# Turning the gates of a gated attention trunk: VectorE blocks and a trip through DRAM in place of TensorE transposes

## The chip, the core and the metric

The kernel runs on one core of a Trainium2 chip. The metric is the device time of one execution in microseconds (us), the median of several. Engines are named as in the profile: PE is TensorE's matmul, PEld its weight load, DVE is VectorE, ACT is ScalarE, POOL is GpSimd, SP is SyncE, which only issues transfers. ACT and POOL issue transfers too.

## The reference, cut to what matters

One layer over 512 tokens of width 2048. A projection of the normalised input gives, for each of three mixers (A, B, C) and four heads of width 128, a query, a key, a value and a gate. Each mixer computes attention in its own way; the head's output is multiplied by SiLU of the gate, projected up, weighted by sigmoid merge gates, summed and projected out.

```
hn = rmsnorm(x, norm_g)
proj = jnp.einsum('bsd,dc->bsc', hn, w_in)
br = proj[..., :QKVG_COLS].reshape(b, s, N_BRANCH, 4, BRANCH_W)      # q, k, v, gate
gates = jax.nn.sigmoid(proj[..., QKVG_COLS + N_HEADS:] + b_gate)
...
ys = jnp.stack([from_heads(ya), from_heads(yb), from_heads(yc)], axis=2)
ys = ys * jax.nn.silu(br[:, :, :, 3])
up = jnp.einsum('bsnw,nwd->bsnd', ys, w_up)
merged = jnp.sum(gates * up, axis=2)
return x + jnp.einsum('bsd,de->bse', merged, w_out)
```

All of it is float32. The shape of the problem: SEQ = 512, D_MODEL = 2048, three mixers of four heads, HEAD_DIM = 128.

## The kernel before, in words

**Products.** Every float32 product is made of three passes of a faster type: an operand is split into a high half and a low half (`wh` and `wl` for weights), and high x high, high x low and low x high are added up in PSUM. ACT makes the high half of a weight tile by a copy (line 377), DVE the low half by a subtraction (line 385). There are three buffers for `wh` (`LA + 1`) and two for `wl` (`LA`). The matmuls of all big products stand on one line, 266.

**Units.** The work on weights is a list of 405 units, each with one weight tile of 128 x 1024 (the first two have half of it) and 12 or 24 matmuls of 128 x 512. The first 9 units are head (C, 0), its weight columns for q, k, v and gate together; the next 8 a group of merge-gate columns. Then come eleven products in Strassen's form (class `Strassen`), 28 units each: each makes one head's 512 columns and one group of merge-gate columns at once, from seven products over half the tokens. Then the up projection and the output projection. A head's four token blocks `c[tb]` (128 tokens on partitions, 512 columns: q, k, v, gate) are there when its product's units end.

**Stages of a head.** Class `Head` makes attention out of `c`: `norms` (query and key norms on ACT), `qk` (query and key turned so that the head dimension is on partitions), `gate`, `values`, scores, softmax or stick-breaking, `silu` (line 1054) and `av`, in which the head's output is multiplied by the gate. `turned(r)` (line 867) makes four 128 x 128 transposes on PE into one PSUM bank of the `att` pool and returns it. `gate` copies that bank to the tile `g` on ACT (line 919). `stages` (line 1105) says how many units behind the end of the head's product each starts: `gate` at 2, `silu` at 12 or 14, or at 4 for the last head, whose attention has no product of a later head beside it.

**Order.** The order of PE, ACT and DVE is written out by a planner at build time (class `Flow`). Each stage is a generator that yields an engine and an estimated cost, an event to wait for, or a number of slots of a buffer pool. The planner keeps a clock for each of the three engines, takes whichever instruction can start first (by due time among equals), and emits it then. Its clock is an estimate; on the chip each instruction waits for its data by semaphores, and each engine runs its list in order. Transfers are estimated by `landing` (line 271). The issuing engine waits in its own queue for a transfer's source and for its buffer. SP has nearly all loads and stores; POOL has the loads that add to a tile (`add_up`); ACT has the first two `x` tiles and the output's stores.

**Pools.** `t2` tiles (128 x 512 float32, `NT = 20` of them) hold `c`, `g`, `y` and most other intermediate tiles. `raw` has 8 weight tiles as they come from DRAM. `att` has four PSUM banks for attention and turning, `acc` four for products.

**The start.** The input is loaded as 16 tiles `x` (128 x 512); tiles 0 and 1 go out on ACT's queue (line 296), the first weights and the other `x` tiles on SP's, in the order written in `loads` (line 1454): x0, w0, x1, w1, x2, x3, w2 and so on, without x0 and x1. PE runs 36 small matmuls (line 429) until the first weight is there. The first unit's `wh` is made by DVE (line 374).

Of the kernel before, what the change touches and what calls it, by code (L numbers as in the profile page):

```python
# [8 lines left out]
F32 = mybir.dt.float32  # L9
# [6 lines left out]
P = 128  # L16
S = 512
# [6 lines left out]
QB = S // P  # L24
# [12 lines left out]
Q, K, V, G = 0, 1, 2, 3  # L37
PE, ACT, DVE = 0, 1, 2
# [26 lines left out]
class Flow:  # L65
# [16 lines left out]
    def give(self, slots, n=1):  # L82
        slots.free += [self.fin] * n
# [71 lines left out]
def act_us(n, x=1):  # L155
    return x * (0.075 + 0.00095 * n)


def dve_us(n, x=1):
    return x * (0.1 + 0.00105 * n)  # L160
# [3 lines left out]
def hybrid_kernel(  # L164
# [13 lines left out]
    nc = tc.nc  # L178
# [5 lines left out]
    tp = ctx.enter_context(tc.tile_pool(name="tp", bufs=NT))  # L184
    sp = ctx.enter_context(tc.tile_pool(name="sp", bufs=8))
    dp = ctx.enter_context(tc.tile_pool(name="dp", bufs=1, space=bass.MemoryType.DRAM))
# [5 lines left out]
    def nm(s):  # L192
        uid[0] += 1
        return f"{s}_{uid[0]}"

    flow = Flow()
    spawn, set_, give = flow.spawn, flow.set, flow.give
    t2s, atts, raws, xps = Slots(NT, KEPT), Slots(4), Slots(NR), Slots(NX)
    accs, wls = Slots(4), Slots(LA)

    def t2(s, dt=F32):
        return tp.tile([P, S], dt, tag="t2", name=nm(s))
# [10 lines left out]
    def f(ap):  # L213
        return ap.bitcast(F32)

    def blk(i):
        return slice(i * P, (i + 1) * P)
# [53 lines left out]
    def landing(ready, kb):  # L271

        line[0] = max(line[0], ready) + 0.5
        line[1] = max(line[1], line[0] + 1.0) + kb / 370.0
        return line[1] + 1.5

    def fetch(to, src, ready, kb):
        nc.sync.dma_start(to, src)
        return Event(landing(ready, kb))
# [6 lines left out]
    def stored(slots, n, kb):  # L286

        slots.free += [landing(flow.fin, kb)] * n
# [2 lines left out]
    nc.scalar.preload_act_table_set("natural_log_exp_and_others")  # L291
    small_in = cp.tile([P, consts.shape[1]], F32, name="small_in")
    nc.sync.dma_start(small_in, consts)  # L293
    x_first = [tp.tile([P, S], F32, tag="t2", name=nm("x")) for _ in range(2)]
    for i in range(2):
        nc.scalar.dma_start(x_first[i], xT[i])
    gn = small_in[:, 0:KT]
    gqk = small_in[:, KT:KT + 4]
    bfc = small_in[:, KT + 4:KT + 5]
# [68 lines left out]
    def prep(u):  # L368
        n = u.shape[0] * S
        u.hi = wp.tile([P] + u.shape, F32R, tag="wh", name=nm("wh"), bufs=LA + 1)  # L370
        yield u.there
        if u is units[0]:
            yield DVE, dve_us(n)
            nc.vector.tensor_copy(u.hi, u.raw)  # L374
        else:
            yield ACT, act_us(n)
            nc.scalar.activation(u.hi, u.raw, AF.Copy)  # L377
        set_(u.ready_hi)
        if u.prev is not None:
            yield u.prev.took  # L380
        yield wls, 1
        set_(u.took)
        u.lo = wp.tile([P] + u.shape, F32R, tag="wl", name=nm("wl"), bufs=LA)
        yield DVE, dve_us(n)
        nc.vector.tensor_sub(u.lo, u.raw, f(u.hi))  # L385
        set_(u.ready)
        u.split_done()
# [30 lines left out]
    raw_ev = [Event() for _ in range(KT)]  # L418
# [7 lines left out]
    xraw, x_in = [None] * KT, [Event() for _ in range(KT)]  # L426
# [389 lines left out]
    class Head:  # L816
# [95 lines left out]
        def gate(self):  # L912
            yield from self.all_there()
            yield t2s, 1
            yield atts, 1
            ps = yield from self.turned(G)
            yield ACT, act_us(S)
            self.t[G] = t2("g")
            nc.scalar.activation(self.t[G], ps, AF.Copy)
            give(atts)  # L920
            set_(self.event(G))
# [520 lines left out]
    def loads():  # L1442
        def x(kt):
            yield t2s, 1
            if kt < 2:
                xraw[kt], x_in[kt].t = x_first[kt], (3.6, 5.2)[kt]
                return
            xraw[kt] = t2("x")
            x_in[kt].t = fetch(xraw[kt], xT[kt], 0.0, 256).t

        def n(i):
            n_in[i].t = fetch(xnat[i // 2][:, i % 2, :], xn[i // NQ, i % NQ], 0.0, 256).t

        order = [("x", 0), ("w", 0), ("x", 1), ("w", 1), ("x", 2), ("x", 3), ("w", 2)] + [("n", i) for i in range(4)]
        order += [("x", 4), ("x", 5), ("w", 3)] + [("n", i) for i in range(4, 8)]
        order += [("x", 6), ("x", 7), ("w", 4)] + [("n", i) for i in range(8, 12)]
        order += [("x", 8), ("x", 9), ("w", 5)] + [("n", i) for i in range(12, 14)]
        for i in range(6, 9):
            order += [("x", 2 * i - 2), ("x", 2 * i - 1), ("w", i)] + [("n", j) for j in (14, 15) if i == 7]
        for kind, i in order:  # L1460
            if kind == "x":
                yield from x(i)
            elif kind == "n":
                n(i)
            else:
                yield from units[i].load()
        for u in units[9:]:
            yield from u.load()
# [4 lines left out]
    def stream():  # L1473
        for i, u in enumerate(units):
            for g, slack in side.pop(i, ()):
                spawn(g(), slack, flow.fin)
            for j in range(LA + 1) if i == 0 else (i + LA,):
                if j < len(units):
                    spawn(prep(units[j]), 2.5, flow.fin)
            yield u.ready_hi  # L1480
            yield from u.mms(u)
            give(wls)
            if u.after is not None:
                spawn(u.after(), 0.0, flow.fin)
# [70 lines left out]
```

## Time and profile before

| | |
|---|---|
| Median of 3 runs | 1306.08 us (1305.84 to 1307.55) |
| The profiled execution's own time | 1305.88 us |
| Its span, first to last instruction | 1304.2 us |
| Granted TensorE clock | 1.000 |
| PE, PEld, DVE, ACT, POOL busy | 100%, 83%, 82%, 58%, 7% of the span |
| Moved by DMA | 278.64 MB, mean 214 GB/s |

The span lies inside the profiled execution's own time, so 1.7 us of it are before the first and behind the last instruction. A busy share is the union of an engine's instructions; matmuls overlap, so their durations add up to more than their busy time. "idle before <-X" is time in which the engine did nothing, and what ended it. ACTq and SPq are the issuing side of ACT and SP; a transfer's time to landing runs from its issue to its semaphore. Rows of a window give its bounds and length, then busy time of PE, PEld, DVE, ACT and POOL, then the granted clock, the DMA engines' share and GB/s.

### The profile page before, as it was taken

The page shows a single profiled execution, that of the slowest core. Times are in us where ns is not written, and L with a number is a line of the kernel's source. Part 1 is how long each engine was busy: PE and PEld are TensorE (multiplying, and loading weights), DVE is VectorE, ACT ScalarE, POOL GpSimd, SP SyncE. Part 2 cuts the span into 40 slices and gives each one's busy share as a digit, 9 for nine tenths or more (in the row PEclk, how much of TensorE's full clock was granted, in tenths as well). Part 3 has the DMA queues.
Part 4 walks back from the last instruction along what each step waited for, and adds up shares of the span by engine and source line. Part 5 has one row for each costly group of instructions (what it writes and reads, how often), then busy time and mean ns, then how long its engine had stood idle before and what let it go on. Part 6 is the DMA issues. An engine that isn't in the chain of part 4 may idle for free.

```text
span 1304.2 us, 17267 instructions
## 1 busy us (share of the span) xinstructions
PE 1299.0 (100%) x5985; PEld 1078.7 (83%) x5985; DVE 1063.9 (82%) x1563; ACT 753.0 (58%) x1270; POOL 91.6 (7%) x116
## 2 busy tenths in 40 slices
PE   9999999999999999999999999999999999999998
PEld 7888888888888888888888888888888888888887
DVE  7966796998989888898886886878879668698767
ACT  7745464664547656566475664666658545463442
POOL 0001000110011101110011100110000000000110
PEclk9999999999999999999999999999999999999999
DMA  9845668887787878878687776867786756738983
GB/s 363 249 130 141 187 200 208 230 217 216 219 233 235 239 228 258 236 229 241 182 234 172 218 207 181 239 154 210 210 274 201 267 188 190 187 87 257 253 243 128
DMA packets 95033, 278.64 MB, mean 214 GB/s; under 512 B 10960, under 2 KB 11104, under 8 KB 94944
## 3 DMA queue, kind: packets, MB, share of 16 engines
q1 hardware_dynamic: 77376, 218.27, 49.4%
q0 software_dynamic: 14976, 54.53, 22.9%
q10 hardware_dynamic: 2592, 4.72, 1.0%
q8 instruction: 47, 0.77, 0.2%
q14 instruction: 42, 0.34, 0.1%
HBM read 257.77 MB, written 19.71 MB: 213 GB/s over the span
## 4 chain that ended last, share of the span: by engine, by line
PE 99%; DMA 0%; DVE 0%; SPq 0%; issue 0%
PE acc L266 93%; PE att L872 1%; PE att L1000 1%; PE att L1090 1%; PE att L262 1%; PE att L1089 1%; PE att L263 1%; PE att L261 1%; PE att L1088 1%; PE att L1338 1%; DMA raw<-in_w_col 0%; DVE s L701 0%; DVE wh L374 0%; SPq L293 0%; PE att L969 0%
## 5 line engine op out<-in xcount | busy, mean ns | idle before, releaser
L377 ACT ACTIVATE wh<-raw 128x1024 fp32r<-128x1024 f32 (+1 forms) x404 | 426.0, 1056 | 377.0 <-PE acc L266 300.4
L385 DVE TENSOR_TENSOR wl<-raw,wh 128x1024 fp32r<-128x1024 f32 (+1 forms) x405 | 493.2, 1219 | 159.5 <-PE acc L266 104.1
L266 PE MATMUL acc<-wh,x 128*128 128x512 f32 x1664 | 432.3, 393 | 0.4 <-DVE wh L374 0.4
L266 PEld LDWEIGHTS acc<-wh,x 128*128 128x128 f32 x1664 | 308.5, 188 | 62.1 <-issue 0.6
L266 PE MATMUL acc<-wh,t 128*128 128x512 f32 x1056 | 271.8, 390 | 0.0
L266 PEld LDWEIGHTS acc<-wh,t 128*128 128x128 f32 x1056 | 197.2, 188 | 40.4
L266 PE MATMUL acc<-wl,x 128*128 128x512 f32 x832 | 230.6, 391 | 0.0
L266 PEld LDWEIGHTS acc<-wl,x 128*128 128x128 f32 x832 | 155.4, 188 | 32.6 <-DVE wl L385 0.2
L266 PE MATMUL acc<-wl,t 128*128 128x512 f32 x528 | 148.7, 392 | 0.0
L282 POOL DMA_DIRECT2D raw<-in_w_col x88 | 76.1, 865 | 870.5 <-ACT wh L377 177.3
L587 DVE TENSOR_TENSOR raw<-raw,raw 128x1024 f32<-128x1024 f32 x104 | 126.5, 1219 | 0.1
L266 PEld LDWEIGHTS acc<-wl,t 128*128 128x128 f32 x528 | 98.2, 188 | 19.9
L266 PE MATMUL acc<-wh,m 128*128 128x512 f32 x448 | 112.9, 389 | 0.0
L266 PE MATMUL acc<-wh,y 128*128 128x512 f32 x384 | 103.1, 390 | 0.0
L266 PEld LDWEIGHTS acc<-wh,m 128*128 128x128 f32 x448 | 84.1, 188 | 17.5
L266 PEld LDWEIGHTS acc<-wh,y 128*128 128x128 f32 x384 | 71.9, 188 | 15.0
L266 PE MATMUL acc<-wl,m 128*128 128x512 f32 x224 | 62.5, 390 | 0.0
L266 PE MATMUL acc<-wl,y 128*128 128x512 f32 x192 | 59.4, 391 | 0.0
L266 PEld LDWEIGHTS acc<-wl,m 128*128 128x128 f32 x224 | 41.9, 188 | 8.8 <-DVE wl L385 0.2
L266 PEld LDWEIGHTS acc<-wl,y 128*128 128x128 f32 x192 | 35.8, 188 | 7.1
L247 ACT ACTIVATE ah<-att 128x512 fp32r<-128x512 f32 (+3 forms) x48 | 20.9, 435 | 33.8 <-PE att L1000 33.8
L1304 DVE TENSOR_TENSOR sg<-acc,sg 128x512 f32<-128x512 f32 x48 | 32.8, 689 | 5.0 <-PE acc L266 2.6
(179 smaller groups left out, 1129.7 us busy)
## 6 DMA issues: line engine op xcount, KB each, us to landing
raw<-in_w_col SPq DMA_DIRECT2D x235, 512.0 KB, 4.5
raw<-in_w_col POOLq DMA_DIRECT2D x88, 512.0 KB, 8.1
raw<-in_w_out SPq DMA_DIRECT2D x40, 512.0 KB, 4.6
raw<-in_w_up SPq DMA_DIRECT2D x24, 512.0 KB, 4.1
sg<-gl SPq DMA_DIRECT2D x48, 256.0 KB, 5.1
xf<-in_xn SPq DMA_DIRECT2D x32, 256.0 KB, 6.7
raw<-in_w_out POOLq DMA_DIRECT2D x16, 512.0 KB, 5.9
gl<-u SPq DMA_DIRECT2D x22, 256.0 KB, 9.8
```

Of the source, the lines that this page charges most:

```text
L247: nc.scalar.activation(hi, src, AF.Copy)
L261: nc.tensor.matmul(ps, lh, rh, start=start, stop=False, skip_group_check=more)
L262: nc.tensor.matmul(ps, lh, rl, start=False, stop=False, skip_group_check=more)
L263: nc.tensor.matmul(ps, ll, rh, start=False, stop=stop, skip_group_check=more)
L266: nc.tensor.matmul(ps, w, x, start=start, stop=stop, skip_group_check=more)
L282: nc.gpsimd.dma_start(to, src, accum_op=ALU.add)
L377: nc.scalar.activation(u.hi, u.raw, AF.Copy)
L385: nc.vector.tensor_sub(u.lo, u.raw, f(u.hi))
L587: nc.vector.tensor_add(to.raw, to.raw, self.raw)
L872: nc.tensor.transpose(ps[:, blk(tb)], self.c[tb][:, blk(r)], identf)
L1000: nc.tensor.transpose(ps[:, blk(i)], self.p[i][:, blk(j)], identf)
L1304: nc.vector.tensor_mul(t, ps[tb], t)
```

## The change: what it does

For all heads but the last, `gate` no longer uses PE and PSUM. DVE transposes the gate's 128 x 128 part of each token block into a tile `gt`; its instruction turns each 32 x 32 piece where it stands, so the sixteen pieces of a block are turned but not moved. SP stores `gt` to a DRAM tile `gd`, laid out by piece row. The planner then waits 12 us of its clock, and ACT issues four loads, one for each 32 partitions of the tile `g`, which pick the pieces so that each comes to its place: 512 pieces of 512 B in the store, 2048 pieces of 128 B in the four loads of a head, 256 KB each way. The planner counts 0.3 us of DVE for each transpose and 0.2 us of ACT for the four loads, and takes `g` to be there 14 us later. The last head goes the old way.

At the start, ACT's queue has `x` tile 0 alone; tile 1 goes on SP's queue at its place in `loads`, behind the first weight tile. The low half of the first weight is made after the low half of `x` tile 0 (`raw_ev[0]`).

```
-    x_first = [tp.tile([P, S], F32, tag="t2", name=nm("x")) for _ in range(2)]
-    for i in range(2):
-        nc.scalar.dma_start(x_first[i], xT[i])
+    x_first = tp.tile([P, S], F32, tag="t2", name=nm("x"))
+    nc.scalar.dma_start(x_first, xT[0])
...
         if u.prev is not None:
             yield u.prev.took
+        else:
+            yield raw_ev[0]
         yield wls, 1
...
         def gate(self):
             yield from self.all_there()
             yield t2s, 1
+            if not self.last:
+                t = t2("gt")
+                for tb in range(QB):
+                    yield DVE, 0.3
+                    nc.vector.transpose(t[:, blk(tb)], self.c[tb][:, blk(G)])
+                self.taken()
+                gd = dp.tile([4 * QB, 32, P], F32, name=nm("gd"))
+                nc.sync.dma_start(gd.rearrange("(t a) r c -> (a r) t c", a=4), t.rearrange("p (t c) -> p t c", t=QB))
+                stored(t2s, 1, 256)
+                yield Event(flow.fin + 12.0)
+                yield t2s, 1
+                yield ACT, 0.2
+                t = self.t[G] = t2("g")
+                for b in range(4):
+                    nc.scalar.dma_start(t[32 * b:32 * (b + 1), :].rearrange("p (n c) -> p n c", c=32),
+                                        gd.rearrange("n r (b c) -> b r n c", c=32)[b])
+                self.event(G).t = flow.fin + 14.0
+                return
             yield atts, 1
             ps = yield from self.turned(G)
...
-            if kt < 2:
-                xraw[kt], x_in[kt].t = x_first[kt], (3.6, 5.2)[kt]
+            if kt == 0:
+                xraw[0], x_in[0].t = x_first, 3.6
                 return
```

## The prediction

> **What bounds it.** I read the page's busy shares and its chain first, then who TensorE waited for, then the waits of the engines that feed it.
>
> ```profile
> PE 1299.0 (100%) x5985; PEld 1078.7 (83%) x5985; DVE 1063.9 (82%) x1563; ACT 753.0 (58%) x1270; POOL 91.6 (7%) x116
> PE 99%; DMA 0%; DVE 0%; SPq 0%; issue 0%
> ```
>
> The chain that ends last is TensorE's own instruction stream, so time falls where that stream gets shorter, as long as nothing starts to hold it up. Who it waited for in all, and who its feeders waited for (us in total, times, longest):
>
> ```profile
> PE att L429 <- DVE mskf L303: 1.1, 1, 1.1
> PE acc L266 <- DVE wh L374: 0.4, 1, 0.4
> ...
> ACT wh L377 <- PE acc L266: 300.4, 190, 5.7
> ACT wh L377 <- DMA raw<-in_w_col: 36.9, 20, 4.4
> ```
>
> TensorE waited twice, both times before its first product. ScalarE, which makes the high half of each weight tile, stood 190 times because all three wh buffers were full, and it could lose 4.4 us to a late weight without TensorE noticing. So a lead of about 4.4 us stands between a feeder's delay and the time.
>
> **What leaves TensorE.** The chain around one gate (start, length, what), and the copy out of PSUM behind it on ScalarE:
>
> ```profile
> 399.98 8.62 PE acc L266 x38
> 408.59 0.44 PE att L872 x4
> 409.03 5.47 PE acc L266 x24
> ...
> 409.07 0.60 ACT L919 ACTIVATE g<-att 128x512 f32<-128x512 f32 x1 [0.76 <-PE att L872]
> ```
>
> Four transposes take 0.44 us of the chain. Eleven of the twelve heads lose theirs: 11 x 0.44 = 4.84 us, all of it on the path that sets the end. This term I trust most: every group of four in the chain has that length.
>
> A rule puts it higher. The same instruction's duration (min/median/max):
>
> ```profile
> L872 PE MATMUL att<-identf,w x66: 270/271/273, 157.2 to 999.8; 128*128 128x128 f32 x66
> ```
>
> The Trainium skill (TensorE: Matmul & The Clock Gate, Part 4: PE-mode transpose) gives about 275 ns for a 128x128 transpose in a kernel's context. The row agrees with it as a duration; by it 44 transposes would be 12.1 us. The chain speaks against using it as a price: in 0.44 us it passes four of them, because each starts before the one ahead has ended.
>
> **What VectorE gets.** Per head four 32x32-block transposes of a 128x128 piece. The trace has none. The nearest rows of that size are a copy with one input and a subtraction with two:
>
> ```profile
> L316 DVE CAST identb<-identf 128x128 bf16<-128x128 f32 x1 | 0.2, 216 | 0.0
> 169.03 0.28 DVE L908 TENSOR_TENSOR vl<-w,vh 128x128 fp32r<-128x128 f32 x1
> ...
> 653.00:665.00 12.00, 12.00 (x57) 9.94 (x56) 11.93 (x21) 9.58 (x29) 2.28 (x3) 1.00 0.84 222
> ...
> 657.35 1.22 DVE L385 TENSOR_TENSOR wl<-raw,wh 128x1024 fp32r<-128x1024 f32 x1
> ...
> 659.97 0.61 PE L266 MATMUL acc<-wl,x 128*128 128x512 f32 x2
> ```
>
> So 4 x 0.22 to 4 x 0.28 = 0.88 to 1.12 us a head; I take 1.12, since all data is f32. In the 12 us around this gate VectorE is busy 11.93 us (fourth figure of the windows row), so the work isn't free there: what is queued behind it, the low half wl of a weight tile, comes that much later. The wl begun at 657.35 is done at 658.57 and used at 659.97, so 1.40 us are in hand; 1.12 leaves 0.28. I cost it at nothing on the path, covered by that lead. If the lead is gone, all 1.12 us show: 12.3 us over 11 heads.
>
> **What ScalarE gets.** It loses 0.60 us (the copy) and issues four loads a head. Rows of issues: one whose pieces are strided as here, with partitions in groups of 32, one plain, and ScalarE's load about 12 us after a gate.
>
> ```profile
> L783 SPq DMA_DIRECT2D lf<-fd x4: 608/614/749, 635.5 to 637.6; - x4
> ...
> 1289.01 0.34 ACTq L1423 DMA_DIRECT2D out<-u  x1
> ...
> 421.00:433.00 12.00, 12.00 (x58) 10.15 (x57) 8.24 (x18) 4.05 (x6) 0.00 (x0) 1.00 1.03 302
> ```
>
> Four issues take 1.36 to 3.0 us; I take 4 x 0.61 = 2.4, as the strided one is nearest. Net of the copy +1.8 us a head, where the planner has 0.2. At 12 us behind the gate ScalarE is busy 4.05 of 12 us, and queued behind the loads are wh splits with 4.4 us of lead: nothing on the path.
>
> The loads also wait for the store to be in DRAM, and hold ScalarE if it isn't. For stores of the same 256 KB, issue to landing is:
>
> ```profile
> DMA to landing us min/median/max: 2.0/5.4/10.5
> ```
>
> The planner leaves 12 us, 1.5 more than the slowest. The store stands in SyncE's queue in front of later weight loads and waits there for the four VectorE transposes, about the wait for wl that those loads have anyway. The gate is wanted late, as one head's copy and its first use show:
>
> ```profile
> L919 ACT ACTIVATE g<-att x1: 599/599/599, 161.9 to 161.9; 128x512 f32<-128x512 f32 x1
> L1062 ACT ACTIVATE y<-g x1: 622/622/622, 191.7 to 191.7; 128x512 f32<-128x512 f32 x1
> ```
>
> There are 29.8 us in between; store and loads at 12 + 10.5 = 22.5 fit in.
>
> **What the DMA engines get.** 512 pieces of 512 B and 2048 of 128 B a head: on each of 16 engines 32 and 128. The trace has 64 B pieces (the lf loads, in a window of 2.3 us where nothing else ran) and 2 KB ones (queue 10; packets, MB, share of 16 engines):
>
> ```profile
> q1 hardware_dynamic: 148, 0.01, 3.8%
> ...
> q10 hardware_dynamic: 2592, 4.72, 1.0%
> ```
>
> That is 0.038 x 16 x 2300 / 148 = 9.5 ns, and 0.010 x 16 x 1304200 / 2592 = 81 ns. In a straight line between them by size 128 B come to 12 ns and 512 B to 26: 128 x 12 + 32 x 26 = 2.4 us of every engine. Bounds: all at 9.5 give 1.5 us, all at 81 give 13.0. I take 2.4, since the 64 B row is nearest. The 12 us after the pause are full already (DMA share 1.03 in the row above), so weights slip by as much, which the 4.4 us of lead hold. From about 28 ns a piece (160 x 28 = 4.5 us) they no longer do.
>
> **The start.** Timeline of the first microseconds, the window behind it, and the tightest later weight:
>
> ```profile
> 1.13 4.02 PE L429 MATMUL att<-mskf 128*128 128x128 bf16 x36 [1.13 <-DVE mskf L303]
> ...
> 4.93 0.43 DVE L374 CAST wh<-raw 128x512 fp32r<-128x512 f32 x1 [0.94 <-DMA raw<-in_w_col]
> 5.39 0.69 DVE L385 TENSOR_TENSOR wl<-raw,wh 128x512 fp32r<-128x512 f32 x1
> 5.51 2.49 PE L266 MATMUL acc<-wh,x 128*128 128x512 f32 x8 [0.36 <-DVE wh L374]
> ...
> 6.40 1.94 ACT L448 ACTIVATE x<-x,small_in 128x512 fp32r<-128x512 f32 x3
> ...
> 8.76 1.99 PE L266 MATMUL acc<-wh,x 128*128 128x512 f32 x8
> ...
> 5.50:10.00 4.50, 4.49 (x18) 3.60 (x19) 4.44 (x8) 3.77 (x6) 0.01 (x1) 1.00 1.04 399
> ...
> 26.04 1.06 ACT L377 ACTIVATE wh<-raw 128x1024 fp32r<-128x1024 f32 x1 [0.22 <-DMA raw<-in_w_col]
> ...
> 27.81 3.79 PE L266 MATMUL acc<-wh,x 128*128 128x512 f32 x16
> ```
>
> The first product waits for the first weight (the copy at 4.93 waited for its DMA). x tile 1 no longer shares the transfers ahead of that weight; its 256 KB at 399 GB/s are 0.66 us, so the weight lands up to 0.66 us sooner. TensorE's warm-up runs until 1.13 + 4.02 = 5.15, so of that only the idle 0.36 can be won. Moving x tile 1 to SyncE's queue puts it after one weight load, and the second weight and all that follow on that queue one issue (about 0.45) later; their transfers then queue behind full engines anyway, and x tile 1 converts by 7.05 for a product at 8.76. The low half of x tile 0 now precedes wl on VectorE: in the old order it ran from 6.00 to 6.75, now it can run from 5.39; wl ends later, about 6.8, for a use at 7.84. The gain lasts only if no later weight binds: the tightest is done at 27.10 for 27.81, 0.71 us, more than 0.36. I take 0.36, with -0.45 (everything one issue late) and +0.66 as bounds.
>
> **Sum.** 4.84 + 0.36 = 5.2 us. The profiled execution took 1305.88 us (span 1304.2, 1.7 around it), 0.2 under the median of 1306.08. 1305.88 - 5.2 = 1300.7; half of the 0.2 added, 1300.8.
>
> **Rivals.** Late wl, the slower side: VectorE has 0.07 of 12 us free at the gate. The planner's new order may put the transposes ahead of a wl whose lead is under 1.12. It decides from 5.2 / 11 = 0.47 us of TensorE waiting a head; at the full 1.12 the time is 1300.7 + 12.3 = 1313.0. Against it: the 1.40 us, and PE rows without one wait for wl. Chance 0.08.
>
> Pieces dear: if short pieces cost like long ones, 13.0 us a head fall into a stretch where the engines are full, 4.4 are covered, and 11 x 8.6 = 95 us come on top: 1395; at 31 ns a piece it comes out even. Against it stands the 9.5 ns row. The Trainium skill (VectorE: DVE Perf Modes, The three transpose paths) warns that a plain DMA that transposes by its strides is 19 times slower than the crossbar's 1309 ns for 128x128: 25 us a block, 100 a head. Here both sides move runs of 32 elements, and no row of this trace shows such a rate. Chance 0.04.
>
> No gain kept: the 0.44 us a head return as small waits, on a late store (10.5 of 12 us in the worst row) or a wh behind it: 1306, within the bound. For it, the full DMA window behind the gates; against it, that ScalarE idles 8 of 12 us there. A weaker form, half kept, is 1303.3. Chance 0.10 for the first.
>
> More than forecast: each removed transpose worth its 271 ns, 11.9 us: 1293.8. Against it, the 0.44 row. Chance 0.03.
>
> **How the numbers follow.** The forecast, from 1299.9 (start at its upper bound, 0.05 us less around each gate) to 1303.3 (half of it lost), has 0.75. Its 1300.8 is the prediction. The range goes down to 1299.0 and up to 1306.0, to take in the case without gain; the dear pieces and the full wl case lie outside with 0.12. A measurement of this kernel tells 0.2%, 2.6 us, from no change: faster means below 1303.5. Faster 0.75 + 0.03 = 0.78, same 0.10, slower 0.08 + 0.04 = 0.12.
>
> **What will show it.** PE instructions 5985 - 44 = 5941, the chain without its 0.44 us pieces of the eleven gates, and still no TensorE wait after the start: that is the main term. VectorE up by 10 to 12 us in 44 transposes. First product near 5.15 instead of 5.51. ScalarE waits for the store none or under 2 us. Wrong would be waits of acc L266 for wl or wh behind the gates, loads on queue 10 whose pieces take 28 ns or more, or a unit between 5 and 30 us that starts later than before.

## The result and the profile after

| | before | after |
|---|---|---|
| Median | 1306.28 us of 6 runs (1305.84 to 1307.55) | 1301.47 us of 6 runs (1300.12 to 1302.68) |
| Profiled execution, span | 1305.88, 1304.2 us | 1301.76, 1300.1 us |

The ratio is 0.9963, with a 95% interval of 0.9953 to 0.9974: faster by 4.8 us, where 5.3 were forecast. The runs of the changed kernel lie 2.6 us apart, those of the old one 1.7.

The page of the changed kernel, its busy shares, its queue 10 and its chain:

```profile
PE 1294.1 (100%) x5941; PEld 1075.1 (83%) x5941; DVE 1069.5 (82%) x1607; ACT 748.2 (58%) x1259; POOL 92.0 (7%) x116
...
q10 hardware_dynamic: 25680, 7.34, 2.3%
...
PE 99%; DMA 1%; DVE 0%; issue 0%; ACT 0%; ACTq 0%
```

TensorE has the 5941 instructions forecast and 4.9 us less to do (1299.0 before); it is still what the time is made of. The new 1% of DMA in the chain is one wait. Who waited for whom (us in total, times, longest):

```profile
PE att L430 <- DVE mskf L302: 1.1, 1, 1.1
PE att L261 <- ACT p L1049: 0.9, 1, 0.9
...
ACT wh L376 <- PE acc L266: 317.6, 203, 5.7
...
ACT wh L376 <- DMA g<-gd: 13.2, 5, 3.4
```

Behind the start, TensorE waits once, for 0.9 us, which it didn't before. In the `g<-gd` row ScalarE's next wh stands five times behind the loads of `g`. Such an idle time holds the issues of the four loads too, and some are put down to another transfer, as here:

```profile
427.97 1.06 ACT L376 ACTIVATE wh<-raw 128x1024 fp32r<-128x1024 f32 x1 [3.01 <-DMA raw<-in_w_col]
430.26 2.04 ACTq L930 DMA_DIRECT2D g<-gd  x4
432.48 1.06 ACT L376 ACTIVATE wh<-raw 128x1024 fp32r<-128x1024 f32 x1 [3.45 <-DMA gl<-s]
```

Of the 3.45 us, 2.04 are issues, and 1.23 are ScalarE's wait for the store, from 429.03 to 430.26. Head by head that wait is 0.7 to 1.3 us in six heads and nothing in the other five. No TensorE row answers to it.

Two pieces of the chain of waits, around that wait and around a gate (start, length, what):

```profile
330.25 10.56 DMA gl<-u
...
340.89 0.29 ACT p L1049
...
341.23 0.50 PE att L261
...
394.98 23.36 PE acc L266 x103
```

The last row runs through the place where the old chain had four transposes of 0.44 us; here are 103 matmuls without a break. The three rows above it are the wait: a transfer `gl` took 10.56 us from its issue to its landing, ScalarE's `p` stood until its tile was free, and the scores product stood behind it.

To see where the time went, I took the first matmul of each unit in both traces. At each of the eleven gates the distance shrinks by 0.46 to 0.49 us, in sum 5.2; the wait at 341 us gives back 1.2 by the next unit. The spans differ by 4.1 us: 5.2 - 1.2 = 4.0, and the rest is scattered. That a gate gives some 0.03 more than its 0.44 is the matmuls behind it: 24 of them took 5.47 us in the old chain, and at the rate of the last row 24 take 5.44. At the start nothing is left in this execution: the second unit began at 8.76 before and begins at 8.79 now, the third at 11.49 and 11.53.

The tile `gt` of the changed kernel (durations min/median/max in ns), and the landing of its stores:

```profile
L920 DVE STREAM_TRANSPOSE gt<-w x20: 303/304/307, 162.7 to 905.3; 128x128 f32<-128x128 f32 x20
...
DMA to landing us min/median/max: 10.3/11.6/12.8
```

The tile `g`, the loads on ScalarE's queue and their landing:

```profile
L930 ACTq DMA_DIRECT2D g<-gd x44: 309/500/608, 75.9 to 925.8; - x44
...
DMA to landing us min/median/max: 1.9/2.9/8.3
```

The timeline of VectorE around the gate at 657 us:

```profile
656.66 0.30 DVE L920 STREAM_TRANSPOSE gt<-w 128x128 f32<-128x128 f32 x1
656.89 1.18 DVE L386 TENSOR_TENSOR wl<-raw,wh 128x1024 fp32r<-128x1024 f32 x1
...
661.84 0.31 DVE L920 STREAM_TRANSPOSE gt<-w 128x128 f32<-128x128 f32 x1
...
666.16 0.30 DVE L920 STREAM_TRANSPOSE gt<-v 128x128 f32<-128x128 f32 x1
```

The planner put the four transposes between other work, over 9.8 us. The wl behind the first began 0.23 us after it. So in this stretch no wl was late by the 1.12 us that the prediction set against a lead of 1.40, but by some 0.23 at a time.

And the start (all engines):

```profile
4.67 0.43 DVE L373 CAST wh<-raw 128x512 fp32r<-128x512 f32 x1 [1.12 <-DMA raw<-in_w_col]
...
5.25 2.77 PE L266 MATMUL acc<-wh,x 128*128 128x512 f32 x8
...
6.26 0.75 DVE L454 SCALAR_TENSOR_TENSOR x<-x,small_in,x 128x512 fp32r<-128x512 f32 x1 [0.49 <-ACT x L449]
...
6.93 1.28 DVE L386 TENSOR_TENSOR wl<-raw,wh 128x512 fp32r<-128x512 f32 x2
7.67 0.84 PEld L266 LDWEIGHTS acc<-wl,x 128*128 128x128 f32 x4
...
7.85 1.10 PE L266 MATMUL acc<-wl,x 128*128 128x512 f32 x4
...
8.79 2.00 PE L266 MATMUL acc<-wh,x 128*128 128x512 f32 x8
```

The first product comes 0.26 us sooner (5.25 for 5.51). Then VectorE stands 0.49 us for `x` tile 1 and converts its low half before it makes the first wl, which so is done about 7.6; the product with it begins at 7.85, as before.

### The profile page after: what moved, and what is told of

Read it like the earlier page. It is cut to its first block, busy times and chain, and to the rows that moved or that the text cites. A ratio compares the mean times of both kernels' runs of the same rounds, so it can differ in the third digit from the quotient of the medians.

```text
span 1300.1 us, 17368 instructions
## 1 busy us (share of the span) xinstructions
PE 1294.1 (100%) x5941; PEld 1075.1 (83%) x5941; DVE 1069.5 (82%) x1607; ACT 748.2 (58%) x1259; POOL 92.0 (7%) x116
## 4 chain that ended last, share of the span: by engine, by line
PE 99%; DMA 1%; DVE 0%; issue 0%; ACT 0%; ACTq 0%
PE acc L266 93%; PE att L1019 1%; PE att L873 1%; DMA gl<-u 1%; PE att L1109 1%; PE att L1108 1%; PE att L261 1%; PE att L262 1%; PE att L263 1%; PE att L1357 1%; PE att L1107 1%; PE att L430 0%; DVE s L702 0%; DVE u L1161 0%; DVE gt L920 0%
```

## The experiments

Theory: the gain is the eleven gates' transposes and nothing else; what was added lies behind leads. Each rival below says that some part of the added work shows, or that the start does. The ratios are to the old kernel, run beside each.

**Start alone, gates alone.** Two kernels, each with one part of the change undone. The first:

```
-            if not self.last:
+            if False:
```

> All twelve gates are turned by TensorE as before; only the order of the first transfers and of the first low halves is that of the change. Theory (the gain is TensorE's removed transposes, and the new start wins nothing because the first product comes 0.26 us sooner but the second unit starts 0.03 us later): the time of before within 1 us, 1305.3 to 1307.3. Rival (the start brings the 0.36 us that the prediction gave it and more behind it): 1305.9 or less with the second unit at 8.4 us instead of 8.76. Rival (most of the gain is the start): under 1303.5.

Measured: 1305.91 us (1305.70 to 1306.79), ratio 0.9998 (0.9989 to 1.0007). TensorE's timeline of this kernel:

```profile
5.04 2.70 PE L266 MATMUL acc<-wh,x 128*128 128x512 f32 x8
...
8.48 1.98 PE L266 MATMUL acc<-wh,x 128*128 128x512 f32 x8
```

Here the second unit is 0.28 us sooner than in the old kernel, and the ninth at 43.84 for 44.13. The other traces of this section bear that out. With the new start the first product comes at 4.99 to 5.25 us in all eleven of them, with the old one at 5.48 to 5.59 in three. The ninth unit starts at 44.08 to 44.19 in those three, and with the new start, leaving out the two kernels that make the first wl sooner, at 43.69 to 43.95 in six of nine. The other three are the changed kernel (44.20), the one with the keys (44.20) and the one without a pause (44.78). So the profiled execution of the changed kernel is one of the few in which the start won nothing; in most, 0.2 to 0.4 us of it are still there at 44 us. The time of the whole can't tell so little: the interval here is 0.9 thousandths, 1.2 us, to either side. The second kernel keeps the new gates:

```
-    x_first = tp.tile([P, S], F32, tag="t2", name=nm("x"))
-    nc.scalar.dma_start(x_first, xT[0])
+    x_first = [tp.tile([P, S], F32, tag="t2", name=nm("x")) for _ in range(2)]
+    for i in range(2):
+        nc.scalar.dma_start(x_first[i], xT[i])
...
-        else:
-            yield raw_ev[0]
...
-            if kt == 0:
-                xraw[0], x_in[0].t = x_first, 3.6
+            if kt < 2:
+                xraw[kt], x_in[kt].t = x_first[kt], (3.6, 5.2)[kt]
```

> The gates of eleven heads go by VectorE and DRAM, the start is that of before. Theory: 11 x 0.47 us less, 1301.1, if no stall comes with the new order of the plan, and up to 1 us more if the wait that the changed kernel has near 341 us comes here too: 1301 to 1302.5. Rival (the start carries the gain): 1304 or more.

Measured: 1301.15 us (1300.53 to 1302.87), ratio 0.9962 (0.9949 to 0.9974). The gates carry the difference; what the start is worth lies below what the times can tell.

**The added work alone.** The old kernel, with its transposes on TensorE and beside them the new path into a tile that nobody reads:

```
+        def side_gate(self):
+            yield t2s, 1
+            t = t2("gt")
+            for tb in range(QB):
+                yield DVE, 0.3
+                nc.vector.transpose(t[:, blk(tb)], self.c[tb][:, blk(G)])
...
+            if not self.last:
+                spawn(self.side_gate(), 5.0)
```

> The kernel before, which keeps TensorE's transposes and uses their result; beside them the VectorE transposes, the store and the four loads of eleven heads are done as in the change, into a tile that nobody reads. So it has all that the change adds and nothing that it removes. Theory (what is added lies beside TensorE's work): the time of before, 1305.5 to 1307.5. Rival (late wl on VectorE, 0.47 us or more a head): 1311.5 or more. Rival (ScalarE's wait for the store and its issues cost 0.1 us a head): about 1307.5.

Measured: 1309.43 us (1307.85 to 1310.69), ratio 1.0022 (1.0012 to 1.0032). Added work costs about 3 us of the median and 4.8 of the profiled execution (span 1309.0 for 1304.2), which is in none of the ranges written down. By unit starts 4.0 of the 4.8 are lost between 340 and 445 us; at most other heads the steps cancel. The chain there:

```profile
338.27 10.01 DMA raw<-in_w_col
...
348.47 0.31 ACTq L927
...
349.90 0.50 ACTq L927
...
350.44 0.29 ACT p L1051
...
350.77 0.50 PE att L261
```

A weight load took 10.01 us, and ScalarE stood 2.42 us for it. Between the wh that it then made and the `p` that TensorE wanted stood the four issues of loads, 348.47 to 350.40, the last 1.0 us of them behind the end of that wh. TensorE waited 2.0 us. So the issues are hidden only where ScalarE is ahead. This kernel also holds more `t2` tiles than the changed one, and no run tells that apart; its loss can't be read as the cost of the change. It shows what the added work can cost when it falls badly.

**The pause.** How much of the 12 us is needed: three kernels with other pauses.

```
-                yield Event(flow.fin + 12.0)
+                yield Event(flow.fin)
```

> The changed kernel without the 12 us that the planner leaves between the VectorE transposes and ScalarE's loads: ScalarE comes to the loads at once and stands in front of them until the store has landed, 10 to 13 us a head by the changed kernel's rows. Theory (about 4 to 5 us of lead stand between ScalarE and TensorE, and the pause keeps the wait inside it): each of eleven heads loses some 12 - 5 = 7 us, but the rest of the gain stays: 1301 + 50 to 90 = 1350 to 1390. Rival (ScalarE's wait costs nothing, since its work can all be made up): within 3 us of 1301.5. Rival (there is no lead, every microsecond counts): 1301 + 11 x 12 = 1433 or more.

Measured: 1439.24 us (1434.54 to 1441.84), ratio 1.1013 (1.0992 to 1.1035), in the range of the dearest rival (1433 or more, no lead at all), far above the theory's 1350 to 1390. Who waited in this kernel:

```profile
PE att L873 <- ACT w L865: 81.9, 10, 12.9
PE acc L266 <- DVE wl L386: 13.2, 4, 7.2
PE att L261 <- ACT p L1049: 9.7, 1, 9.7
...
ACT w L865 <- DMA g<-gd: 106.5, 7, 16.1
```

And one of its stretches (bounds and length, busy PE, PEld, DVE, ACT, POOL, then the granted clock, DMA share, GB/s):

```profile
440.00:462.00 22.00, 10.71 (x50) 8.59 (x48) 8.21 (x17) 4.19 (x9) 1.73 (x2) 0.82 0.98 278
```

Directly behind the gate, what is queued behind the loads on ScalarE is the head's own norm scaling (line 865), and TensorE's turning of keys and queries comes at once after it: there the lead is about zero. TensorE stands for 115 us in all (span 1438.0, busy 1323.1). In and after such stands the granted clock is lower (0.82 in this stretch; 1.00 in the same one of the changed kernel), and its busy time is 29 us longer, 1323.1 for 1294.1. Some 20 us of that are longer distances between matmuls of line 266, most of them 427 ns where 227 is usual.

```
-                yield Event(flow.fin + 12.0)
+                yield Event(flow.fin + 7.0)
```

> The changed kernel with a pause of 7 us. ScalarE then stands some 5 to 6 us a head for the store, 5 us more than in the changed kernel, and later in the head than with no pause. Theory (a lead of 4 to 5 us for the weight splits, which is what stands behind the loads at that place): near the edge, 0 to 2 us a head, 1301 to 1323. Rival (every microsecond of ScalarE's wait shows, as without a pause): 11 x 5 more, 1350 or more. Rival (hidden altogether): within 1 us of 1301.5.

Measured: 1310.99 us (1310.49 to 1311.79), ratio 1.0034 (1.0021 to 1.0048). TensorE's and ScalarE's waits:

```profile
PE acc L266 <- ACT wh L376: 5.0, 3, 1.9
...
ACT wh L376 <- DMA g<-gd: 46.9, 7, 9.1
```

This is in the theory's range. Now wh splits are behind the loads, as the prediction had it, and of 46.9 us of standing (some 2 us of issues in each of the seven) 5.0 reach TensorE. Most of the rest of the 8.7 us of span is longer busy time (1298.6 for 1294.1, +4.5): 1.7 of it are ten slow matmuls behind one of the three waits, on which more below, and the remainder is scattered.

```
-                yield Event(flow.fin + 12.0)
+                yield Event(flow.fin + 16.0)
```

> The changed kernel with a pause of 16 us in place of 12 between the transposes on VectorE and ScalarE's loads. In the changed kernel ScalarE stands 1 to 2.5 us for the store in most heads; with 16 us it shouldn't. Theory (those waits are hidden): 1301.5 within 1 us. Rival (they cost 0.1 us a head or more): 1300.4 or less.

Measured: 1301.10 us (1300.08 to 1304.74, the highest alone above 1301.2), ratio 0.9963 (0.9949 to 0.9977): the same as with 12 us. ScalarE has no row left that waits for the store. So the waits for `g` in the changed kernel were hidden, and the pause is worth some 9.5 us from 7 to 12, and nothing from 12 to 16.

**The store on ScalarE's queue.** The store lands after 10.3 to 12.8 us though its pieces need about 1 us of each engine. Is that time spent behind the weight loads of SyncE's queue?

```
-                nc.sync.dma_start(gd.rearrange("(t a) r c -> (a r) t c", a=4), t.rearrange("p (t c) -> p t c", t=QB))
+                yield ACT, 0.4
+                nc.scalar.dma_start(gd.rearrange("(t a) r c -> (a r) t c", a=4), t.rearrange("p (t c) -> p t c", t=QB))
```

> The changed kernel with the store of the turned gate on ScalarE's queue instead of SyncE's (the planner counts 0.4 us of ScalarE for it). Question: why the store took 10.3 to 12.8 us to land. Theory (it stands behind weight loads of the same queue): it lands in 3 to 6 us, as the loads of pieces on ScalarE's queue do (median 2.9), and ScalarE no longer waits for it; the time stays within 1.5 us of 1301.5, as those waits were hidden. Rival (512 B pieces are what makes it slow): it lands in 10 us or more here too. Rival (those waits cost part of the gain): 1300 or less.

Measured: 1302.79 us (1302.12 to 1303.52), ratio 0.9973 (0.9963 to 0.9983). Issue and landing of the store in this kernel:

```profile
L924 ACTq DMA_DIRECT2D gd<-gt x11: 382/382/389, 63.2 to 911.2; - x11
...
DMA to landing us min/median/max: 11.6/12.8/14.2
```

It lands later, not sooner. In the records of single pieces, leaving out the first head, a store's first piece starts 3.6 to 3.9 us after the issue (in the changed kernel 7.5 to 10.1), and its last at 11 to 13.5; there the 512 pieces are through in 2 to 6 us, here they take 7 to 10. The engines are near full in either case: other transfers take 0.86 to 0.99 of them in the 13 us behind an issue. So SyncE's queue is where the store waits in the changed kernel, but ScalarE's queue only moves the wait in between the pieces: 32 pieces on each engine over 8.7 us are one every 0.27 us on average, ten times the 27 ns that one takes. The Trainium skill (DMA: Bandwidth & Descriptors, Queues, rings and completion order) says that an engine goes round the queues it has work for and switches at packet boundaries. That would put other transfers in between; the records don't name the engine of a piece, and no run here isolates it.

**The start's other half.** The rival for the lost 0.36 us was that a later weight binds; the trace also shows the first wl behind `x` tile 1. Here that tile's low half waits for the first weight:

```
+            if kt == 1:
+                yield units[0].ready
```

> The changed kernel, but VectorE makes the low half of the first weight before the low half of x tile 1, not after it. Theory (the start's gain was lost because wl of unit 0 was done at 7.62 us when TensorE wanted it at about 7.5, since VectorE had first waited 0.49 us for x tile 1): the second unit starts near 8.5 instead of 8.79, about 0.3 us less in all, with the same stall near 341 us if the plan keeps it: 1300.5 to 1301.5. Rival (a later weight binds, so that the start can't gain): second unit sooner, but the unit near 27 us starts no sooner than now, 1301.5.

Measured: 1300.54 us (1300.34 to 1301.60), ratio 0.9958 (0.9945 to 0.9970). TensorE's timeline:

```profile
7.95 1.98 PE L266 MATMUL acc<-wh,x 128*128 128x512 f32 x8
...
11.03 1.21 PE L266 MATMUL acc<-wh,x 128*128 128x512 f32 x4 [0.20 <-ACT wh L376]
```

The second unit is 0.84 us sooner (7.95 for 8.79). Then TensorE waits 0.2 us for a wh at 11.03, 0.3 later for another, and the sixth unit starts at 27.99 (27.85 in the changed kernel), the ninth at 44.45 (44.20). What this order wins is gone within some 20 us: a later weight binds. That this kernel is 0.9 below the changed one is within the runs' spread; its trace has no wait at 341 us, which may be a part of it.

**The wait at 341 us.** The planner frees a tile that is stored as `gl` at an estimated landing; the transfer took 10.56 us. Two kernels free such tiles 5 us later, the first all of them:

```
-        stored(t2s, 1, 256)
+        t2s.free += [landing(flow.fin, 256) + 5.0]
```

> The changed kernel, but the planner counts 5 us more before the tiles whose merge-gate columns go to DRAM are free again. Theory (the one TensorE wait behind the start, 0.95 us near 341 us, comes from a scores tile of head (C, 3) planned into the place of a tile whose store was still under way, 10.6 us after its issue): that wait is gone, no other comes in its place, 1 us less: 1299.8 to 1301. Rival (the wait has another cause, ScalarE's loads of the gate or the pieces): it stays, 1301.5. Rival (fewer free tiles make the plan tighter elsewhere): 1302.5 or more with new waits.

Measured: 1304.54 us (1303.38 to 1305.55), ratio 0.9986 (0.9976 to 0.9995). TensorE's wait is gone, but what was behind it is not. ScalarE's `p` still stands for the store:

```profile
339.59 0.94 ACT L1049 ACTIVATE p<-att 128x128 f32<-128x128 f32 x3 [1.70 <-DMA gl<-u]
```

And another wait has come, near the last head (TensorE's timeline):

```profile
1018.96 1.47 PE L266 MATMUL acc<-wh,y 128*128 128x512 f32 x4 [1.51 <-DVE sg L1323]
...
1021.08 1.91 PE L266 MATMUL acc<-wh,y 128*128 128x512 f32 x4
...
1024.81 1.07 PE L266 MATMUL acc<-wh,y 128*128 128x512 f32 x4
```

Between 997 and 1026 us it loses 4.6 us, by this wait and by matmuls at a lower rate behind it (1.91 us for four where 1.07 is usual). So the later freeing was kept for the first eleven column groups only:

```
-        stored(t2s, 1, 256)
+        t2s.free += [landing(flow.fin, 256) + (5.0 if i < NB * NQ - 1 else 0.0)]
```

> As the run in which the planner counts 5 us more for the stores of merge-gate columns, but for the first eleven column groups only, so that the plan of the last head and of the up projection isn't touched (there the earlier run lost 4.6 us between 997 and 1026 us). Theory (the 0.95 us wait near 341 us is a planned-in wait for such a store, and only the new plan of the last head cost time): no wait near 341 us, units 325 to 328 as in the changed kernel, 0.7 to 1.2 us less than the changed kernel: 1300 to 1301. Rival (the gain in the middle can't be had without a loss elsewhere): 1301.5 or more, with a new wait.

Measured: 1301.75 us (1301.00 to 1302.89), ratio 0.9966 (0.9952 to 0.9980). TensorE has no wait at 341 us and a span of 1299.3, 0.8 below the changed kernel's; the median isn't lower. But the later freeing isn't what took the wait away. In ten of the kernels with the new gates, these two among them, `p` waits for the semaphore of the same store, issued near 330 us (334 with the pause of 7 us); what differs is when it lands. `p` started 10.64 us behind the issue in the changed kernel and 11.45 in the one with the store on ScalarE's queue, and TensorE stood 0.95 and 1.75 us. In the other eight it started 9.13 to 9.80 behind it, and TensorE stood 0.10 us or not at all; five of these eight have no later freeing. So the late store is the cause, and the planner's early place for `p` makes the kernel open to it; that freeing 5 us later helps is not shown. What the wait is worth lies within the spread of the runs.

**More of the same: keys too.** Keys of the seven heads of the first two mixers that aren't the last go the way of the gates, with a pause of 16 us for both, and scores start two units later:

```
+            far = not self.last and self.n != C
+            far = far and r in (K,)
+            if far:
+                yield t2s, 1
+                ps = yield from self.round_trip(r, "kq", 16.0, 6.0)
...
-                s, t, o = (OFF["s1"], OFF["t1"], OFF["o1"]) if self.last else (OFF["s"], OFF["t"], OFF["o"])
+                s, t, o = (OFF["s1"], OFF["t1"], OFF["o1"]) if self.last else (OFF["s"] + 2, OFF["t"] + 2, OFF["o"] + 2)
```

> The changed kernel, and besides the gates also the keys of seven heads (mixers A and B, all but the last head) go by VectorE and DRAM, with a pause of 16 us for both; the scores and what follows come 2 units later in these heads. Theory (what counts is the number of transposes taken from TensorE, 0.47 us for four, while the pieces, the issues on ScalarE and VectorE's work stay hidden): 7 x 0.47 = 3.3 us less than the changed kernel, 1297.5 to 1299. Rival (the transfers behind a head's end are full, and a second round trip there is late: ScalarE or the scores wait): 1301 or more, with TensorE waits for ScalarE or for weights 10 to 30 us behind the gates of A and B.

Measured: 1324.96 us (1323.4 to 1330.1), ratio 1.0140 (1.0123 to 1.0157). Its waits, a piece of its chain, and the stretch behind that piece:

```profile
PE acc L266 <- DVE wl L386: 12.0, 6, 2.7
PE att L261 <- ACT qkh L899: 7.0, 2, 4.6
```

```profile
708.21 12.70 DMA kq<-gd
...
722.49 0.47 PE att L262
```

```profile
726.00:737.00 11.00, 11.00 (x46) 8.94 (x45) 5.71 (x15) 7.39 (x14) 0.00 (x0) 0.87 0.41 131
```

The profiled execution is the slowest of the four. Keys are wanted soon after they are there; the last load alone took 12.70 us in this piece, its issue included, behind the pause. Some 20 us of waiting come on top of the changed kernel's, and TensorE is busy 8.3 us longer (1302.4) with 28 instructions fewer, at a granted clock of 0.87 behind the wait. The edit also starts the scores later and gives ScalarE's issues 1.9 us of the plan, and no run has these alone, so the share of the keys' own lateness isn't shown. The waits for qkh and this chain fit the reading that gates can go this way because they are wanted late.

**The three mendings together.** First wl sooner, pause 16, later freeing in the first eleven groups:

> The changed kernel with all three edits that took a wait away when made alone: x tile 1's low half waits for unit 0's wl, the pause is 16 us instead of 12, and the planner counts tiles stored as gl as free 5 us later in the first eleven column groups. Theory (what is left is TensorE's own stream): no TensorE wait after the start, the third unit no earlier than 11.0 us since it waits for its wh, and a time of 1299.8 to 1301.3, which the changed kernel's 1301.47 can't be told from. Rival (the planner's new order makes a wait elsewhere, as the free 5 us later did near the end): one wait of TensorE of 1 us or more and 1302.0 or above. Second rival (the three add up, 0.9 of the start, 1.2 of the wait at 341 us and some tenths for the stores): 1299.3 or below.

Measured: 1300.60 us (1300.03 to 1300.86), ratio 0.9955 (0.9942 to 0.9969). The one row of TensorE's waits:

```profile
PE att L430 <- DVE mskf L302: 1.1, 1, 1.1
```

The time is in the theory's range, and TensorE waits for nothing behind the start; the third unit came at 10.78, sooner than the 11.0 expected, as the first product did too (5.02). Against the changed kernel the second unit is 0.95 us ahead and the seventh 0.41. Its interval overlaps that of the changed kernel, so it can't be called faster.

## Why the prediction was right, and where it wasn't

**What leaves TensorE** (11 x 0.44 = 4.84 us): right. Measured 0.46 to 0.49 a gate, 5.2 in sum, and with the gates alone the whole difference. The case of 0.271 us for each transpose (the Trainium skill, TensorE: Matmul & The Clock Gate, Part 4: PE-mode transpose, has about 275 ns) fell: the group's length in the chain was the price, not the sum of durations.

**What VectorE gets**: the size was off, the result held. A transpose took 0.30 us, above both bounds (0.22 and 0.28); four are 1.22 us, not 1.12. The figure of the Trainium skill (VectorE: DVE Perf Modes, The three transpose paths), 311 ns for bf16, was nearer than my rows, and the f32 here agrees with it. The lead of 1.40 us against a block of 1.12 was the wrong picture: the planner spread the four out, and around the gate looked at a wl came some 0.23 us later. The sign "VectorE up by 10 to 12 us" failed: its busy time rose by 5.6 (1063.9 to 1069.5), though the 44 durations add up to 13.3. Busy time counts each moment once, however many instructions overlap in it, so it rises by less than the durations of what is added.

**What ScalarE gets**: the issues were 0.50 us at the median, four of them about 2.0 a head (2.4 taken, 1.36 to 3.0 bounds). Two steps failed. The store's landing, bounded at 10.5 us by other stores of its size, was 10.3 to 12.8: full engines, and its queue's weight loads ahead of it. So ScalarE waited for it, up to 1.3 us, where the sum had no wait. That is still within the sign "none or under 2 us", and it was hidden, as the 16 us pause shows. And "queued behind the loads are wh splits with 4.4 us of lead" holds for the place where the pause puts the loads, not as a property of ScalarE: with no pause the lead there was about zero (1439 us), with 7 us it was overrun (1311).

**What the DMA engines get**: right. Queue 10's share rose from 1.0% of 1304.2 us to 2.3% of 1300.1, about 270 us over 16 engines for 23088 more packets, 11.7 ns each (12 forecast; the records of single pieces give 11 to 13 ns for 128 B and 27 for 512 B, where 26 was forecast). The dear pieces of the 1395 us case didn't come.

**The start** (0.36 us): failed in the profiled execution, where the second unit starts at 8.79 for 8.76, one of the signs of being wrong. The first product did come sooner, by 0.26 us, but the step "The low half of x tile 0 now precedes wl on VectorE", by which "wl ends later, about 6.8", left out `x` tile 1, whose low half also went first: wl ended at 7.6. In the other traces with the new start and this order of low halves it ended at 7.2 to 8.3, also later than 6.8; yet in six of these eight the ninth unit came 0.2 to 0.4 us sooner than in the old kernel's trace. So the size may be about right, and no time confirms it. The claim that no later weight binds, since the tightest had 0.71 us, failed beyond that: with the first wl sooner, wh rows bind at 11 us and later.

**What wasn't foreseen**: the wait of 0.95 us at 341 us. The forecast's upper end, 1303.3, allowed for a loss of that size but named no mechanism for it: the planner's new order puts a tile where a store isn't done if that takes more than some 10 us to land. The sum of what was mis-sized, in this execution: +0.36 not won, 0.36 more at the gates (5.2 for 4.84), about 1 lost at 341; the median is 0.7 above the forecast, within the spread of the runs.

## What to carry to other kernels

Price an instruction that leaves a full engine by its piece in the chain, not by its duration, and expect it back only if what replaces it is wanted late: the same move for keys, with the scores moved later, cost some 23 us where gates won 4.8. A lead read from a wait belongs to the place in the order where it was seen, so look up what stands behind the new instruction there. A plan made from estimates re-orders with every change, so leave room for a wait of a microsecond somewhere far from the edit. And before an edit is said to have taken a wait away, look whether the instruction still waits for the same thing.

## What the runs showed of the hardware that I hadn't expected

Short stands of TensorE can cost more than themselves. With the pause of 7 us, TensorE stood 1.93 us (its timeline):

```profile
185.39 2.90 PE L266 MATMUL acc<-wh,x 128*128 128x512 f32 x8 [1.93 <-ACT wh L376]
188.09 1.91 PE L266 MATMUL acc<-wl,x 128*128 128x512 f32 x4
189.79 1.12 PE L266 MATMUL acc<-wh,x 128*128 128x512 f32 x4
```

From 186.8 to 189.4 us seven matmuls came 426 ns apart, where 227 is usual; the granted clock is 0.50 there, and 0.91 over 180 to 200 us. The stand of 1.51 us near 1019 us above, with one of 0.33 two us earlier, has the like behind it, and 0.50 too. The two other stands of the kernel with 7 us, 1.45 and 1.6 us, had none, and neither had those of 1.75 us (the store on ScalarE's queue) and 1.98 (the added work alone). The Trainium skill (TensorE: Matmul & The Clock Gate, Why this matters for your kernels) warns of idle gaps over about 3 us; here the half rate followed gaps of 1.5 and 1.9 us, but not one of 1.98, so length alone doesn't decide. What does wasn't tried.

A small store that was taken off the queue with the weight loads didn't land sooner, with the engines 0.86 to 0.99 full of other transfers (12.8 us for 11.6 at the median).
